# An encoder layer on one core: squares and the rotary sine product moved from GpSimd to VectorE, softmax rows handled in pairs

## The chip, the cores and the metric

The kernel runs on one core of a Trainium2 chip. The metric is the device time of one execution in microseconds, the median of the runs shown. One further execution was taken by the hardware profiler; its own time stands beside them.

## What is computed

One layer of a bidirectional encoder over 1024 tokens of width 1024, in float32. Cut to what matters:

```python
hn = rmsnorm(x, norm_mix)
qa, ka, va, qb, kb, vb = split(hn @ w_in)         # 8+2+2 heads for group A, 8+8+8 for group B, 64 wide
qa, ka = partial_rope(qa), partial_rope(ka)       # the first 16 of 64 dims are rotated
# group A: sliding window |i-j| <= 128, 4 query heads share a key head, one learned sink logit per head
m = max(max(s), sink); p = exp(s - m); denom = sum(p) + exp(sink - m); o_a = p @ va / denom
# group B: neighbourhood attention on a 16 x 64 token grid, window 8 x 16, learned bias by offset
p = softmax(s + bias); o_b = p @ vb
h = x + concat(rmsnorm(o_a, norm_a), rmsnorm(o_b, norm_b)) @ w_out
hn = rmsnorm(h, norm_ffn)
h = h + (silu(conv3(hn @ w_gate)) * (hn @ w_up)) @ w_down      # conv3: centred, depthwise, width 3; 2816 wide
out = rmsnorm(h, norm_final)
```

## The kernel before

Activations lie transposed in SBUF: features on the 128 partitions, the 1024 tokens along the free axis, eight tiles of 128x1024 for a width of 1024. Every matmul operand is split into a high and a low part (ScalarE rounds the high part, VectorE subtracts it), and each product is three matmuls: high by high, low by high, high by low (`block`, lines 113 to 115). Half a tile of 512 tokens is one bank of PSUM.

**Start (0 to 45 us).** The tiles of x arrive one by one. `split_scaled` makes `xgh` (line 125, ScalarE) and `xgl` (line 126, VectorE). Two projections run over all eight tiles as they come; their four accumulators fill four banks. `load_w` loads weights and splits them (lines 108 and 109). The sum of the squares of x, for the first RMS norm, comes from `squares(xts, nc.gpsimd)`: ScalarE squares a tile (line 139) and the engine that is named adds it to the sum (line 141), seven adds of 128x1024. A third projection starts before the norm is known. Then the partition sums (line 150), the inverse root and its spreading over all partitions (`widen`, line 161) give `rstd1`, by which every projection is multiplied when it leaves its bank (`evacuate`, line 170).

**Projections and attention (45 to 400 us).** Each projected tile goes through `post`. The tiles of group A's queries and keys (six of them) are rotated by `rotate`: two DMAs issued from ScalarE's queue copy the partner rows into a tile `u` (line 182; two such tiles take turns), VectorE multiplies the tile by the cosines (line 183), GpSimd multiplies `u` by the sines (line 184), and VectorE adds the two (line 185). `split_pair` (lines 190 to 195) then makes the two query operands, with three DMAs on SyncE's queue, and `split_k` the keys.

Attention goes by rows: one row is one head's 128 queries against 256 or 384 keys. `scores` makes two matmuls (line 266) into one of two banks named `s`. `softmax` follows: GpSimd copies the negated sink logit into a spare column (line 283, group A alone), VectorE subtracts the scores from the mask or bias, writes them into `p` and finds the row's extremum (line 284), ScalarE takes the exponential and its sum (line 288), VectorE inverts the sum (line 289), GpSimd scales the row (line 290). Two rows share one tile `p`. Then TensorE transposes `p` (line 322 in group A, 395 in group B), ScalarE and VectorE split the transposed tile into `ph` and `pl` (lines 295, 296), and TensorE multiplies them with the values (lines 327 and 328, or 406 and 407). In group A a unit has the four heads of one key head at one block, 16 units in all; in group B a unit has two rows, 32 units.

**The order.** TensorE's order is written out by hand. The score rows run up to two units ahead of the transposes, and between these steps `fill` puts in blocks of the projections that later units need, at rates that a table `RATES` sets. The order on the other engines is made by a scheduler at build time from dependencies and priorities; `softmax` runs at raised priority. Each engine then executes its list in that order.

**Output projection and MLP (400 to 1135 us).** These use TensorE, VectorE and ScalarE, and GpSimd four times at the very end.

Of the kernel before, what the change touches and what calls it, by code (L numbers as in the profile page):

```python
# [13 lines left out]
F32 = mybir.dt.float32  # L14
F32R = mybir.dt.float32r
AF = mybir.ActivationFunctionType
ALU = mybir.AluOpType
# [34 lines left out]
def hybrid_layer(tc, xT, w_in, w_out, w_gate, w_up, w_down, small, sink, rpb, consts, rope, out):  # L52
    nc = tc.nc
    with ExitStack() as ctx:
# [9 lines left out]
        spool = inner("stats", 6)  # L64
# [6 lines left out]
        def tmp(name, dt=F32, n=S):  # L71
            return tpool.tile([128, n], dt, name=name, tag="t", padded_shape=[128, S + 2])
# [62 lines left out]
        def squares(tiles, engine):  # L135
            acc = None
            for t in tiles:
                s2 = tmp("sq")
                nc.scalar.activation(s2, t, AF.Square)
                if acc is not None:  # L140
                    engine.tensor_tensor(s2, s2, acc, op=ALU.add)
                acc = s2
            return acc
# [34 lines left out]
        def rotate(t, n):  # L178
            u = turned[0]
            turned.append(turned.pop(0))  # L180
            for i in (0, 4):
                nc.scalar.dma_start(u[i:n:8], t[4 - i:n:8])
            nc.vector.tensor_tensor(t[0:n], t[0:n], rc[0:n], op=ALU.mult)
            nc.gpsimd.tensor_tensor(u[0:n], u[0:n], rs[0:n], op=ALU.mult)
            nc.vector.tensor_tensor(t[0:n], t[0:n], u[0:n], op=ALU.add)

        def split_pair(t):
# [86 lines left out]
                return lpool.tile([128, 2, 386], F32, name="p", tag="mix", bufs=slots["mix"], padded_shape=[128, 2, 512])  # L274
            return apool.tile([128, 2, 386], F32, name="p", tag="p", bufs=5)

        def softmax(p, j, ps, n, bias, nsink=None):

            w = lambda ap: ap.rearrange("p (c w) -> p c w", w=128)
            with tc.high_priority(offset=50):  # L280
                nm, sm = spool.tile([128, 1], F32, name="nm"), spool.tile([128, 1], F32, name="sm")
                if nsink is not None:
                    nc.gpsimd.tensor_copy(p[:, j, n:n + 1], nsink)
                nc.vector.tensor_tensor_reduce(  # L284
                    out=w(p[:, j, 0:n]), in0=w(ps[:, 0:n]), in1=bias, scale=1.0, scalar=3e38 if nsink is None else nsink,
                    op0=ALU.add, op1=ALU.min, accum_out=nm)
                e = n if nsink is None else n + 1
                nc.scalar.activation(p[:, j, 0:e], p[:, j, 0:e], AF.Exp, bias=nm, scale=-1.0, accum_out=sm)  # L288
                nc.vector.reciprocal(sm, sm)  # L289
                nc.gpsimd.tensor_scalar(p[:, j, 0:n], p[:, j, 0:n], sm, 1.0, op0=ALU.mult, op1=ALU.mult)  # L290

        def split_pt(ps, n):
            ph = apool.tile([128, HALF], F32R, name="ph", tag="ph")
# [5 lines left out]
        def unit_window(g, b):  # L299

            cs, n = near(b), 128 * len(near(b))
            ps4 = [None] * 4
            mask = cst[:, K_MA:K_MA + 384].rearrange("p (c w) -> p c w", w=128)
            mask = mask[:, cs[0] - b + 1:cs[-1] - b + 2]
            st = {}

            def q_step(j):
                def go():
                    if j % 2 == 0:
                        st["p"] = pair_tile(True)  # L310
                    ps, _ = scores(qa[g, j // 2][j % 2], ka[g], b)
                    softmax(st["p"], j % 2, ps, n, mask, nsink[:, 4 * g + j:4 * g + j + 1])
                    ps4[j] = st["p"][:, j % 2, :]
                return go

            def t_step(i):
                def go():
                    if i == 0:
                        st["o"] = bank("o", "o")
                    pt = bank("pt", "pt")  # L320
                    for j in range(4):
                        nc.tensor.transpose(pt[:, j * 128:(j + 1) * 128], ps4[j][:, i * 128:(i + 1) * 128], ident)
                    ph, pl = split_pt(pt, HALF)

                    def v_step():
                        o, v = st["o"], va[g]
                        nc.tensor.matmul(o, v[:, cs[i], :], ph, start=i == 0, stop=False)
                        nc.tensor.matmul(o, v[:, cs[i], :], pl, start=False, stop=i == len(cs) - 1)
                        if i == len(cs) - 1:
                            leave()  # L330
                    return v_step
                return go

            def leave():
                ot = apool.tile([128, 2, 128], F32, name="ot", tag="ot", bufs=1, padded_shape=[128, 4, 128])
                o4 = st["o"][:, :].rearrange("p (j w) -> p j w", w=128)
                for e in range(2):
                    me, other = slice(64 * e, 64 * e + 64), slice(64 - 64 * e, 128 - 64 * e)
                    nc.scalar.activation(ot[me], o4[other, e::2, :], AF.Copy)
                    for i in range(2):  # L340
                        if mix[2 * g + i] is None:
                            mix[2 * g + i] = big("mixa", "mix")
                        nc.vector.tensor_tensor(mix[2 * g + i][me, b * 128:(b + 1) * 128], o4[me, e + 2 * i, :], ot[me, i, :], op=ALU.add)

            return [q_step(j) for j in range(4)], [t_step(i) for i in range(len(cs))]
# [19 lines left out]
        def units_grid(h):  # L365

            ps4 = [None] * NB
            st = {"begun": [False, False]}
            e = 64 * (h % 2)
            me, other = slice(e, e + 64), slice(64 - e, 128 - e)  # L370

            def q_step(b):
                def go():
                    if b == 0:
                        bias_of[h] = bias_of.pop(h, None) or bias_tiles(h)
                    if b == 4 and h < 7:
                        bias_of[h + 1] = bias_tiles(h + 1)
                    x = bias_of[h]
                    if b % 2 == 0:
                        st["p"] = pair_tile()  # L380
                    sel = slice(2, 5, 2) if b == 0 else slice(0, 3, 2) if b == NB - 1 else slice(1, 4)
                    ps, n = scores(qb[h], kb[h], b)
                    softmax(st["p"], b % 2, ps, n, x[:, sel, :])
                    ps4[b] = st["p"][:, b % 2, :]
                return go

# [111 lines left out]
        xts, sqs = [], []  # L498
# [42 lines left out]
        nsink = cpool.tile([128, 8], F32, name="nsink")  # L541
        nc.vector.tensor_scalar(nsink, par[:, C_SINK:C_END], -1.0, None, op0=ALU.mult)
        rc, rs = big("rc", "mix"), big("rs", "mix")
# [3 lines left out]
        for _ in range(2):  # L547
            u = big("u", "mix")
# [4 lines left out]
        acc = None  # L553
        for k in range(KT):
            if k:
                xg[k] = split_scaled(xts[k], col(C_NMIX + k), "xg", "xg")
            for h in range(2):
                for p, ps in zip(first, banks):
                    block(ps[h], p.w[k], xg[k], h, k == 0, k == KT - 1)
        acc = squares(xts, nc.gpsimd)  # L560
        jobs = [Project(m) for m in range(2, 18)] + [OutA(d) for d in range(KT)]
        third = jobs[0]
        raw, hi, lo = big("raw3", "mix"), big("whi3", "mix", F32R), big("wlo3", "mix", F32R)
# [184 lines left out]
        for h in range(2):  # L748
            wide = widen(vb2[h], "pt")
            for i in range(4):  # L750
                x = mix[4 + i][:, tsl(h)]
# [93 lines left out]
        for h in range(2):  # L845
            for d in range(KT):
                if h == 0 and d + 2 < KT:
                    wo.append(load_wo(d + 2, fpool))
                ps = bank("pj", ("pj", "o", "s")[(h * KT + d) % 3])
# [264 lines left out]
        for i, f in enumerate(FO[HEAD:]):  # L1114
            u = Gated(f)
# [99 lines left out]
        for i, (p, j, c) in enumerate(order):  # L1215
            prepare(i + 6, i + 4)
            f, n = PARTS[c]
# [4 lines left out]
            ps = banks[p, j]  # L1222
# [120 lines left out]
```

## Time and profile before

| | |
|---|---|
| timed runs | 1141.33 us median of 3 (1141.04 to 1143.16) |
| the profiled execution | 1136.96 us, its span 1135.0 us |
| mean granted TensorE clock | 0.986 of full speed |
| GpSimd: squares, line 141 | 7 adds, 19.6 us |
| GpSimd: sine products, line 184 | 6 products, 16.9 us |
| GpSimd: scaling of rows, line 290 | 128 passes, 77.4 us |
| GpSimd: copies of the sink, line 283 | 64 copies, 13.3 us |
| VectorE: reciprocals, line 289 | 128, 20.1 us |

The span runs from the first to the last instruction of the profiled execution; all durations are from that execution. PE is TensorE, PEld its weight loads, DVE is VectorE, ACT ScalarE, POOL GpSimd, SP SyncE. A timeline row gives the start in us, the duration, engine, line, operation, the tile written and the tiles read, the shape, and in brackets how long the engine stood idle before it and what ended that. A row of grouped instructions has the count, then busy time and the mean of one in ns, then the idle time before. Matmuls overlap in the pipe, so their starts are closer together than their durations are long.

### The profile page before, as it was taken

The numbers are of one execution on the slowest core, as the hardware profiler recorded it, in microseconds if no ns is written. First come the engines' busy times: TensorE is split into PE (matmuls) and PEld (weight loads), VectorE is DVE, ScalarE is ACT, GpSimd is POOL, SyncE is SP. The second block draws the span as 40 slices with busy tenths as digits, with TensorE's granted clock in tenths as the row PEclk, the third lists the DMA queues.
The fourth block names the chain that finished last, engine by engine and source line by source line (L and its number), as shares of the span: only waits on it lengthen the run. The fifth ranks groups of instructions, "written<-read, shape, count | busy, mean of one in ns | idle before, by whom it ended". The sixth has DMA issues, their size and how long they took to land.

```text
span 1135.0 us, 15044 instructions
## 1 busy us (share of the span) xinstructions
PE 1088.1 (96%) x5124; PEld 903.0 (80%) x5124; DVE 874.7 (77%) x1594; ACT 550.2 (48%) x1033; POOL 149.1 (13%) x233
## 2 busy tenths in 40 slices
PE   7989999999999989999899999999999899999995
PEld 5867788888878878888688888888888688888884
DVE  6687888766689667899988778877887778886843
ACT  6235677655767534445443334333433554543531
POOL 4634533233223100000000000000000000000001
PEclk8999999999999999999999999999999999999998
DMA  7242120233305317402542223222322799775723
GB/s 273 72 119 74 48 57 28 73 95 89 78 28 150 101 47 241 146 31 96 192 131 103 107 89 129 94 103 93 123 101 93 232 319 298 260 226 163 261 78 148
DMA packets 65294, 147.17 MB, mean 130 GB/s; under 512 B 7969, under 2 KB 14113, under 8 KB 65217
## 3 DMA queue, kind: packets, MB, share of 16 engines
q1 hardware_dynamic: 56256, 121.17, 34.1%
q10 hardware_dynamic: 8960, 25.04, 5.8%
q8 instruction: 40, 0.66, 0.2%
q14 instruction: 38, 0.30, 0.1%
HBM read 104.37 MB, written 28.57 MB: 117 GB/s over the span
## 4 chain that ended last, share of the span: by engine, by line
PE 82%; DVE 8%; DMA 3%; issue 3%; ACT 2%; POOL 1%; SPq 0%; POOLq 0%; ACTq 0%; DVEq 0%
PE dn L785 6%; PE dn L786 6%; PE dn L787 6%; PE pj L113 6%; PE pj L114 6%; PE pj L115 6%; PE z L785 5%; PE z L787 5%; PE z L786 5%; PE x L785 3%; PE x L786 3%; PE x L787 3%; PE y L787 3%; PE y L785 3%; PE y L786 3%; PE s L266 3%
## 5 line engine op out<-in xcount | busy, mean ns | idle before, releaser
L774 ACT ACTIVATE whi<-ws 128x512 fp32r<-128x512 f32 (+1 forms) x100 | 60.1, 623 | 125.4 <-DVE ws L891 85.5
L785 PE MATMUL dn<-xd,whi 128*128 128x512 f32 x308 | 120.0, 390 | 0.0
L787 PE MATMUL dn<-xd,wlo 128*128 128x512 f32 x308 | 119.8, 389 | 0.0
L786 PE MATMUL dn<-xd,whi 128*128 128x512 f32 x308 | 119.8, 389 | 0.0
L785 PE MATMUL z<-hg,whi 128*128 128x512 f32 x264 | 103.4, 392 | 2.4 <-DVE gs L941 2.4
L787 PE MATMUL z<-hg,wlo 128*128 128x512 f32 x264 | 103.7, 393 | 0.2 <-DVE wlo L775 0.2
L113 PE MATMUL pj<-xgh,whi 128*128 128x512 f32 x248 | 103.8, 418 | 0.0
L786 PE MATMUL z<-hg,whi 128*128 128x512 f32 x264 | 103.3, 391 | 0.0
L290 POOL TENSOR_SCALAR p<-p,sm 128x384 f32<-128x384 f32 (+1 forms) x128 | 77.4, 606 | 192.1 <-DVE sm L289 165.3
L1197 POOL TENSOR_TENSOR y<-y,wide 128x512 f32<-128x512 f32 x4 | 5.1, 1280 | 734.1 <-ACT y L1196 734.1
L288 ACT ACTIVATE p<-p,nm 128x385 f32<-128x385 f32 (+3 forms) x128 | 74.9, 586 | 49.4 <-DVE nm L284 43.9
L114 PE MATMUL pj<-xgl,whi 128*128 128x512 f32 x248 | 97.8, 394 | 0.3 <-DVE xgl L126 0.3
L115 PE MATMUL pj<-xgh,wlo 128*128 128x512 f32 x248 | 98.1, 396 | 0.0
L775 DVE TENSOR_TENSOR wlo<-raw,whi 128x512 fp32r<-128x512 f32 (+1 forms) x102 | 66.5, 671 | 22.1 <-ACT whi L774 21.1
L774 ACT ACTIVATE whi<-raw 128x512 fp32r<-128x512 f32 (+1 forms) x102 | 61.0, 612 | 46.3 <-DMA raw<-in_w_down_dram 11.1
L775 DVE TENSOR_TENSOR wlo<-ws,whi 128x512 fp32r<-128x512 f32 (+1 forms) x100 | 66.9, 681 | 19.8 <-ACT whi L774 19.7
L296 DVE TENSOR_TENSOR pl<-pt,ph 128x384 fp32r<-128x384 f32 (+2 forms) x108 | 63.2, 588 | 21.5 <-ACT ph L295 20.2
L295 ACT ACTIVATE ph<-pt 128x384 fp32r<-128x384 f32 (+2 forms) x108 | 55.3, 514 | 40.6 <-PE pt L395 29.4
L1098 ACT ACTIVATE xd<-xd 128x512 fp32r<-128x512 f32 x77 | 46.9, 626 | 54.1 <-DMA xd<-x 50.7
L787 PE MATMUL y<-hg,wlo 128*128 128x512 f32 x176 | 69.4, 394 | 2.2 <-DVE wlo L775 2.2
L785 PE MATMUL y<-hg,whi 128*128 128x512 f32 x176 | 69.1, 393 | 1.9 <-ACT whi L774 1.9
L785 PE MATMUL x<-hg,whi 128*128 128x512 f32 x176 | 68.8, 391 | 1.4 <-ACT c L925 1.4
(201 smaller groups left out, 2721.9 us busy)
## 6 DMA issues: line engine op xcount, KB each, us to landing
xd<-x SPq DMA_DIRECT2D x77, 256.0 KB, 4.9
raw<-in_w_down_dram SPq DMA_DIRECT2D x72, 256.0 KB, 3.5
raw<-in_w_gate_dram SPq DMA_DIRECT2D x22, 512.0 KB, 3.4
raw<-in_w_up_dram SPq DMA_DIRECT2D x22, 512.0 KB, 5.6
x<-c ACTq DMA_DIRECT2D x22, 512.0 KB, 2.9
raw<-in_w_in_dram SPq DMA_DIRECT2D x32, 256.0 KB, 2.7
raw<-in_w_down_dram SPq DMA_DIRECT2D x36, 192.0 KB, 3.9
x<-t ACTq DMA_DIRECT2D x11, 512.0 KB
```

The source lines that it names most:

```text
L113: nc.tensor.matmul(ps, w[0], x[0][:, tsl(h)], start=first, stop=False)
L114: nc.tensor.matmul(ps, w[0], x[1][:, tsl(h)], start=False, stop=False)
L115: nc.tensor.matmul(ps, w[1], x[0][:, tsl(h)], start=False, stop=last)
L288: nc.scalar.activation(p[:, j, 0:e], p[:, j, 0:e], AF.Exp, bias=nm, scale=-1.0, accum_out=sm)
L290: nc.gpsimd.tensor_scalar(p[:, j, 0:n], p[:, j, 0:n], sm, 1.0, op0=ALU.mult, op1=ALU.mult)
L295: nc.scalar.activation(ph[:, 0:n], ps[:, 0:n], AF.Copy)
L296: nc.vector.tensor_tensor(pl[:, 0:n], ps[:, 0:n], f32(ph[:, 0:n]), op=ALU.subtract)
L774: nc.scalar.activation(hi, src, AF.Copy)
L775: nc.vector.tensor_tensor(lo, src, f32(hi[:, :, :]), op=ALU.subtract)
L785: nc.tensor.matmul(ps, w[0], x[0], start=first and i == 0, stop=False, skip_group_check=True)
L786: nc.tensor.matmul(ps, w[0], x[1], start=False, stop=False, skip_group_check=True)
L787: nc.tensor.matmul(ps, w[1], x[0], start=False, stop=last and i == len(ws) - 1, skip_group_check=True)
```

## The change

The adds of x's squares and the sine product go to VectorE. In `softmax` the two rows that share a tile `p` also share a tile for the sums, 128x2: the sink column of both is copied at once, and when the second row's exponential is done, one reciprocal inverts both sums and GpSimd scales both rows, one after the other.

```diff
@@ -181,7 +181,7 @@
             for i in (0, 4):
                 nc.scalar.dma_start(u[i:n:8], t[4 - i:n:8])
             nc.vector.tensor_tensor(t[0:n], t[0:n], rc[0:n], op=ALU.mult)
-            nc.gpsimd.tensor_tensor(u[0:n], u[0:n], rs[0:n], op=ALU.mult)
+            nc.vector.tensor_tensor(u[0:n], u[0:n], rs[0:n], op=ALU.mult)
             nc.vector.tensor_tensor(t[0:n], t[0:n], u[0:n], op=ALU.add)
 
         def split_pair(t):
@@ -274,20 +274,26 @@
                 return lpool.tile([128, 2, 386], F32, name="p", tag="mix", bufs=slots["mix"], padded_shape=[128, 2, 512])
             return apool.tile([128, 2, 386], F32, name="p", tag="p", bufs=5)
 
-        def softmax(p, j, ps, n, bias, nsink=None):
+        def softmax(st, j, ps, n, bias, nsink=None):
 
             w = lambda ap: ap.rearrange("p (c w) -> p c w", w=128)
+            p = st["p"]
             with tc.high_priority(offset=50):
-                nm, sm = spool.tile([128, 1], F32, name="nm"), spool.tile([128, 1], F32, name="sm")
-                if nsink is not None:
-                    nc.gpsimd.tensor_copy(p[:, j, n:n + 1], nsink)
+                nm = spool.tile([128, 1], F32, name="nm")
+                if j == 0:
+                    st["sm"], st["n"] = spool.tile([128, 2], F32, name="sm"), [n, n]
+                sm, st["n"][j] = st["sm"], n
+                if nsink is not None and j == 0:
+                    nc.gpsimd.tensor_copy(p[:, 0:2, n:n + 1], nsink.rearrange("p (j o) -> p j o", o=1))
                 nc.vector.tensor_tensor_reduce(
-                    out=w(p[:, j, 0:n]), in0=w(ps[:, 0:n]), in1=bias, scale=1.0, scalar=3e38 if nsink is None else nsink,
+                    out=w(p[:, j, 0:n]), in0=w(ps[:, 0:n]), in1=bias, scale=1.0, scalar=3e38 if nsink is None else nsink[:, j:j + 1],
                     op0=ALU.add, op1=ALU.min, accum_out=nm)
                 e = n if nsink is None else n + 1
-                nc.scalar.activation(p[:, j, 0:e], p[:, j, 0:e], AF.Exp, bias=nm, scale=-1.0, accum_out=sm)
-                nc.vector.reciprocal(sm, sm)
-                nc.gpsimd.tensor_scalar(p[:, j, 0:n], p[:, j, 0:n], sm, 1.0, op0=ALU.mult, op1=ALU.mult)
+                nc.scalar.activation(p[:, j, 0:e], p[:, j, 0:e], AF.Exp, bias=nm, scale=-1.0, accum_out=sm[:, j:j + 1])
+                if j == 1:
+                    nc.vector.reciprocal(sm, sm)
+                    for i, m in enumerate(st["n"]):
+                        nc.gpsimd.tensor_scalar(p[:, i, 0:m], p[:, i, 0:m], sm[:, i:i + 1], 1.0, op0=ALU.mult, op1=ALU.mult)
 
         def split_pt(ps, n):
             ph = apool.tile([128, HALF], F32R, name="ph", tag="ph")
@@ -309,7 +315,7 @@
                     if j % 2 == 0:
                         st["p"] = pair_tile(True)
                     ps, _ = scores(qa[g, j // 2][j % 2], ka[g], b)
-                    softmax(st["p"], j % 2, ps, n, mask, nsink[:, 4 * g + j:4 * g + j + 1])
+                    softmax(st, j % 2, ps, n, mask, nsink[:, 4 * g + j - j % 2:4 * g + j - j % 2 + 2])
                     ps4[j] = st["p"][:, j % 2, :]
                 return go
 
@@ -380,7 +386,7 @@
                         st["p"] = pair_tile()
                     sel = slice(2, 5, 2) if b == 0 else slice(0, 3, 2) if b == NB - 1 else slice(1, 4)
                     ps, n = scores(qb[h], kb[h], b)
-                    softmax(st["p"], b % 2, ps, n, x[:, sel, :])
+                    softmax(st, b % 2, ps, n, x[:, sel, :])
                     ps4[b] = st["p"][:, b % 2, :]
                 return go
 
@@ -557,7 +563,7 @@
             for h in range(2):
                 for p, ps in zip(first, banks):
                     block(ps[h], p.w[k], xg[k], h, k == 0, k == KT - 1)
-        acc = squares(xts, nc.gpsimd)
+        acc = squares(xts, nc.vector)
         jobs = [Project(m) for m in range(2, 18)] + [OutA(d) for d in range(KT)]
         third = jobs[0]
         raw, hi, lo = big("raw3", "mix"), big("whi3", "mix", F32R), big("wlo3", "mix", F32R)
```

## The prediction

> **What bounds the kernel now.** I read the busy times and the chain of waits on the page first, then the table of stretches, then the timeline where TensorE idles.
>
> ```profile
> PE 1088.1 (96%) x5124; PEld 903.0 (80%) x5124; DVE 874.7 (77%) x1594; ACT 550.2 (48%) x1033; POOL 149.1 (13%) x233
> PE 82%; DVE 8%; DMA 3%; issue 3%; ACT 2%; POOL 1%; SPq 0%; POOLq 0%; ACTq 0%; DVEq 0%
> 20.00:30.00 10.00, 7.56 (x31) 5.25 (x31) 10.00 (x5) 5.44 (x7) 7.43 (x4) 1.00 0.62 220
> 160.00:180.00 20.00, 20.00 (x107) 17.11 (x106) 17.25 (x52) 13.78 (x34) 7.39 (x22) 1.00 0.32 80
> 480.00:1135.00 655.00, 634.51 (x2803) 523.81 (x2801) 510.99 (x765) 275.38 (x443) 5.12 (x4) 0.99 0.45 151
> ```
>
> A row of stretches has the length, then the busy time of TensorE, its weight loads, VectorE, ScalarE and GpSimd, then the granted clock, the DMA share and GB/s. TensorE sets the end, at 96%. Its order is written out by hand and is the same, instruction for instruction, in the changed kernel as built. So the change can only fill or open holes on TensorE. Nothing that it edits runs behind 480 us: that block shifts as a whole. The holes within its reach are in the first 30 us (VectorE busy 10.00 of 10.00 from 20 to 30), around 77 us, and in the attention; by 160 to 180 there are none.
>
> **The squares.** VectorE gets seven adds of 128x1024. Before, GpSimd made them beside VectorE's splits of x (line 126).
>
> ```profile
> L141 DVE TENSOR_TENSOR sq<-sq x3: 1215/1226/1228, 285.5 to 290.5; 128x1024 f32<-128x1024 f32 x3
> 11.64 1.28 DVE L126 SCALAR_TENSOR_TENSOR xgl<-xt,par,xgh 128x1024 fp32r<-128x1024 f32 x1 [1.84 <-ACT xgh L125]
> 12.63 12.01 POOL L141 TENSOR_TENSOR sq<-sq 128x1024 f32<-128x1024 f32 x4 [11.66 <-ACT sq L139]
> 16.17 2.88 DVE L109 TENSOR_TENSOR wlo<-raw,whi 128x512 fp32r<-128x512 f32 x1
> 18.97 7.94 DVE L126 SCALAR_TENSOR_TENSOR xgl<-xt,par,xgh 128x1024 fp32r<-128x1024 f32 x3
> 26.84 0.68 DVE L109 TENSOR_TENSOR wlo<-raw,whi 128x512 fp32r<-128x512 f32 x1
> ```
>
> And TensorE's idles in the same stretch (start, duration, and in brackets the idle before it and who ended that):
>
> ```profile
> 20.51 0.39 PE L113 MATMUL pj<-xgh,w 128*128 128x512 f32 x1
> 22.44 0.50 PE L114 MATMUL pj<-xgl,w 128*128 128x512 f32 x1 [1.54 <-DVE xgl L126]
> 25.77 0.50 PE L114 MATMUL pj<-xgl,whi 128*128 128x512 f32 x1 [0.32 <-DVE xgl L126]
> 27.57 0.51 PE L115 MATMUL o<-xgh,wlo 128*128 128x512 f32 x1 [0.58 <-DVE wlo L109]
> ```
>
> A split takes 1.28 us when GpSimd is still idle and 7.94 / 3 = 2.65 us beside a GpSimd add; line 109 takes 0.68 alone and 2.88 beside one. Here the two engines slow each other down, GpSimd's adds included: 12.01 / 4 = 3.0 us each. On VectorE an add costs 1.23 us (the row at 285 us). In the order as built, the queue from 11.64 on is split, add, split, line 109, add, split: 1.28 + 1.23 + 1.28 + 0.68 + 1.23 + 1.28 = 7.0 us, so the third split ends near 18.6 to 19. Before, it ended at 18.97 + 2.65 = 21.6, and TensorE wanted it at about 20.7, right behind the row of 20.51. After it come an add and the next two splits, 3.8 us, to about 22.8; TensorE wants the first of them near 23.5. So the three idles go: 1.54 + 0.32 + 0.58 = 2.44 us. Each also made the matmul behind it 0.11 us longer (0.50 against 0.39): 2.44 + 0.33 = **2.8 us**. The last three adds stand behind the last split. Even if that ended no earlier than before (about 32 us), they would be done by 32 + 3.7 = 36 us; the sum of squares is needed only at about 40 (42.9 in the next fence, less 2.8), so these adds are covered.
>
> **The rotation's sine product.** Six products move to VectorE, each right behind the cosine product. The first three are on the way to the first queries:
>
> ```profile
> 42.90 0.95 PE L150 MATMUL ss<-ones,sq 128*128 128x1 f32 x8
> 52.99 5.79 POOL L184 TENSOR_TENSOR u<-u,rs 64x1024 f32<-64x1024 f32 x2 [5.01 <-DMA u<-t]
> 56.47 3.40 DVE L185 TENSOR_TENSOR t<-t,u 64x1024 f32<-64x1024 f32 x1 [1.05 <-POOL u L184]
> 62.13 1.21 DVE L185 TENSOR_TENSOR t<-t,u 128x1024 f32<-128x1024 f32 x1
> 64.47 2.22 DVE L192 SCALAR_TENSOR_TENSOR t<-t,q 128x1024 fp32r<-128x1024 f32 x1 [0.53 <-ACT q L190]
> 72.81 2.37 POOL L184 TENSOR_TENSOR u<-u,rs 64x1024 f32<-64x1024 f32 x1 [7.21 <-DMA u<-t]
> 73.69 2.57 DVE L183 TENSOR_TENSOR t<-t,rc 64x1024 f32<-64x1024 f32 x1
> 77.00 1.21 DVE L185 TENSOR_TENSOR t<-t,u 64x1024 f32<-64x1024 f32 x1
> 78.17 0.48 DVE L284 CUSTOM_DVE_ANT_0 p<-s,cst,nsink 128x256 f32<-128x256 f32 x1
> 77.66 0.36 PE L266 MATMUL s<-ka,q 128*128 128x256 f32 x1 [3.33 <-DMA q<-t]
> 78.72 0.44 PE L266 MATMUL s<-ka,q 128*128 128x384 f32 x1 [0.35 <-DVE nm L284]
> ```
>
> A product costs 1.21 on VectorE (the add at 62.13 has its shape), against 5.79 / 2 = 2.9 on GpSimd, and the add behind it no longer runs beside a product (3.40). The first tile's addition ends at 59.87 now. On VectorE it ends, in the old time scale, at 52.99 + 3 x 1.21 for cosine product, sine product and addition + 0.68 for an eviction of 128x512 between them (the shape of line 109's 0.68) = 57.3: some 2.5 us sooner. A new wait comes with this: the product needs the rows that ScalarE's DMA queue copies into u, and all of VectorE's work stands behind it (evictions, splits, score rows), for which TensorE's banks wait. The rows had landed by 52.99 and VectorE comes to them at about 54.2, behind the cosine product, so it doesn't stop. The rows of the fourth tile land at 72.81, about 70 after the change, and are reached at about 73 (below).
>
> So the DMA of the query tile, which TensorE awaits for 3.33 us at 77.66, lands earlier by 2.8 plus about 2, part of the 2.5 and the 1.0 that line 192 gains (2.22 at 64.47 beside a product), while TensorE arrives 2.8 earlier: this wait shrinks to about 2.3. But it gives nothing, because a new wait stands right behind it. As built, VectorE's queue goes: score rows 0 and 1, cosine product, sine product, addition, row 2; before, the cosine product stood ahead of row 0 and no sine product was there. Rows 0 and 1 cannot start before TensorE's scores at about 73.7 - 2.8 = 70.9 (the 73.69 row began as these ran). Then 2 x 0.41 for the rows, 3 x 1.17 for the three vector passes (77.00 to 78.17, start to start) and 0.41 for row 2: 70.9 + 0.3 + 0.8 + 3.5 + 0.4 = 75.9. TensorE's next scores need the bank that row 2 frees: 78.72 before, 75.9 after, 2.8 us sooner. The whole gain of the squares is kept, and of the faster rotation **0 to 0.5 us**, I take 0.2.
>
> The clock has a part here:
>
> ```profile
> 75.40:78.80 3.40, 0.80 (x5) 0.62 (x5) 3.40 (x10) 1.65 (x5) 0.00 (x0) 1.00 0.36 77
> 78.80:82.20 3.40, 3.40 (x10) 2.77 (x11) 2.98 (x11) 2.09 (x7) 2.11 (x3) 0.56 0.35 77
> ```
>
> Behind 3.40 us in which TensorE was busy for 0.80 the granted clock is 0.56 for 3.4 us, which loses 1.5 us. After the change, two waits of about 2.3 and 2 us stand with 0.5 us of scores between them, as empty as now: I leave this loss in. The Trainium skill, "TensorE: Matmul & The Clock Gate", section "What's actually happening", has the clock fall after at least one idle window of about 3.4 us. By that rule two shorter waits with work between would not trigger it, and the loss would go. The trace does not bear out so strict a reading, since 0.80 us of work did not prevent it.
>
> **The later products.** Two run inside the attention.
>
> ```profile
> 115.58 3.46 POOL L184 TENSOR_TENSOR u<-u,rs 128x1024 f32<-128x1024 f32 x1
> 119.08 1.23 DVE L185 TENSOR_TENSOR t<-t,u 128x1024 f32<-128x1024 f32 x1 [1.17 <-POOL u L184]
> ...
> 100.73 0.41 PE L266 MATMUL s<-ka,q 128*128 128x384 f32 x1 [0.43 <-DVE nm L284]
> 121.47 0.50 PE L328 MATMUL o<-pl,v 128*128 128x512 f32 x1 [1.41 <-DVE pl L296]
> 125.82 0.50 PE L328 MATMUL o<-pl,v 128*128 128x512 f32 x1 [1.03 <-DVE pl L296]
> ```
>
> At 119.08 VectorE waits 1.17 for GpSimd; that wait becomes 1.2 us of work, so the wait at 121.47 stays or grows by about 0.6. Ahead of the one at 125.82 the order as built takes one score row out of the way, and row 10, for which TensorE waits at 100.73, moves ahead of two larger passes. Bounds: all three waits go (2.9 us gained), or the first one doubles (1.4 lost). Nearest are the rows themselves: -0.6 + 1.0 + 0.4 = **0.8 us** gained.
>
> **Rows in pairs.** 64 reciprocals of 128x2 replace 128 of 128x1, and 32 copies of the sink replace 64.
>
> ```profile
> L289 DVE RECIPROCAL sm<-sm 128x1 f32<-128x1 f32 x128 | 20.1, 158 | 16.4 <-ACT p L288 15.0 <-POOL p L283 0.2
> L154 DVE RECIPROCAL v<-v 128x4 f32<-128x4 f32 x2 | 0.3, 173 | 3.6 <-ACT v L153 3.6
> PE pt L322 <- POOL p L290: 0.2, 1, 0.2
> 137.40 0.59 POOL L290 TENSOR_SCALAR p<-p,sm 128x384 f32<-128x384 f32 x1
> 139.13 0.60 PE L322 MATMUL pt<-cst,p 128*128 128x128 f32 x4
> ```
>
> A 128x2 reciprocal is not in the trace; it lies between 158 and 173 ns, so VectorE saves 128 x 0.158 - 64 x 0.17 = 9 us, spread over 300 us in which TensorE waits for VectorE only a few times. Of the nine, 0 to 1.5 us can show; I take 0.5. The price is delay: the pair's first row is scaled only when the second one's exponential is done, so the last row of a unit has another pass of 0.59 us ahead of it on GpSimd. TensorE's transposes have cover for that: at 139.13, among the tightest, they begin 139.13 - 137.99 = 1.14 us after a scaled row that the unit's end needs, and in all the attention TensorE waited for a scale once, for 0.2 us. The delay is hidden there with 0.5 us to spare. The pair's reciprocal also holds VectorE's queue until the second exponential is done. Now that is 15.0 us in all, and with half the reciprocals, as many of them close behind their row, no more than that.
>
> **The sum.** 2.8 + 0.2 + 0.8 + 0.5 = 4.3 us. The profiled execution took 1136.96 (span 1135.0 and 1.96 around it) and should take 1132.7. The median of the timed runs, 1141.33, lies 4.4 above it; the same gain gives **1137.0**. What a measurement of this kernel can tell from no change is about 0.2%, 2.3 us; the three runs shown span 2.1.
>
> **The rivals.**
> *The clock stays full behind the first scores* (0.15). The two new waits have 0.5 us of scores between them, and if that keeps the clock up, or the 3.4 us stretches fall otherwise, 1.5 us more are gained: 1135.5. For it: the wait is cut in two; against: the 0.80 us of work in the row above did not help. By the Trainium skill's page on the clock gate this is the outcome.
> *VectorE takes it back* (0.20). It has 7 x 1.23 + 6 x 1.21 = 15.9 us more to do by 120 us. Against it, the splits alone give back 7 x 1.1. If in the order as built it is late once more, as behind row 1, for the length of two passes (2 x 1.2), and the 0.5 of the pairs does not show: 4.3 - 2.9 = 1.4 gained, 1139.9, no change that can be told.
> *The pairs' delay reaches TensorE* (0.22). GpSimd runs in order; scale passes now come in pairs behind copies that wait for a free tile. Where the cover of a unit's last row is under 0.59 us, TensorE stops for its transposes. It decides if VectorE's pair reciprocals come half a microsecond later than the single ones did, because 1.14 is then eaten. For the 14 window units behind the first two (an estimate), at 0.59 each, that is 8.3 us lost: 1141.33 - 4.3 + 8.3 = 1145.3, slower. For it: VectorE is busy 17.25 of 20 there. Against: the one wait of 0.2.
>
> **How the numbers follow.** The forecast has 0.43; its own range, from the bounds of 0.8 and 0.5 and the 1.5 of the clock, is 1134.5 to 1139.5. Faster by over 0.2% (below 1139.05) are the forecast and the first rival, 0.58; within are the second rival, 0.20; slower is the third, 0.22. The range goes from 1133.5 (first rival with the better bounds) to 1144.5, most of the way into the third rival.
>
> **What would show it.** Right: the splits of x at 1.28 with no idle on TensorE between 20 and 28 us; the first score matmuls near 71; the wait there put down to VectorE's row 2; the products at 1.2 on VectorE; the transposes' waits for line 290's scale still near zero. Wrong: waits of the transposes for GpSimd in most window units, waits of the value matmuls for pl that add up to more than before, or a second stretch at half clock.

## The result, and the profile after

The changed kernel took 1134.65 us (median of six runs, 1133.01 to 1138.03) against 1141.3 for the kernel before (six runs): ratio 0.9947, 95% interval 0.9932 to 0.9963, faster by more than the 0.2%. The forecast was 1137.0. The profiled execution took 1133.92, with a span of 1132.1. In a second series the ratio was 0.9962 (0.9947 to 0.9978). The mean of both, 0.9955, is 5.2 us of 1140, against 4.3 forecast.

The busy times, the chain of waits and the stretches of the changed kernel (columns as in the prediction):

```profile
PE 1088.7 (96%) x5124; PEld 905.5 (80%) x5124; DVE 865.2 (76%) x1543; ACT 550.1 (49%) x1033; POOL 110.6 (10%) x188
PE 87%; DVE 7%; DMA 2%; issue 1%; ACT 1%; SPq 0%; POOL 0%; POOLq 0%; ACTq 0%; DVEq 0%
20.00:30.00 10.00, 10.00 (x46) 8.29 (x45) 7.62 (x9) 5.27 (x7) 2.67 (x4) 1.00 0.66 241
160.00:180.00 20.00, 20.00 (x108) 17.15 (x107) 16.70 (x46) 14.56 (x35) 6.29 (x16) 1.00 0.27 69
480.00:1135.00 655.00, 631.42 (x2787) 520.99 (x2786) 509.71 (x762) 273.56 (x440) 5.11 (x4) 0.98 0.44 150
```

VectorE got thirteen large passes more and is yet busy for 9.5 us less. From 20 to 30 us TensorE is busy for 10.00 where it was 7.56. VectorE's timeline shows why:

```profile
11.72 1.28 DVE L126 SCALAR_TENSOR_TENSOR xgl<-xt,par,xgh 128x1024 fp32r<-128x1024 f32 x1 [1.97 <-ACT xgh L125]
15.25 0.69 DVE L109 TENSOR_TENSOR wlo<-raw,whi 128x512 fp32r<-128x512 f32 x1
18.18 1.22 DVE L141 TENSOR_TENSOR sq<-sq 128x1024 f32<-128x1024 f32 x1
19.32 2.48 DVE L126 SCALAR_TENSOR_TENSOR xgl<-xt,par,xgh 128x1024 fp32r<-128x1024 f32 x2
28.36 3.94 DVE L141 TENSOR_TENSOR sq<-sq 128x1024 f32<-128x1024 f32 x3
```

Every split of x takes 1.28 (2.65 before), line 109 takes 0.69 (2.88), an add of the squares 1.22 (3.0 on GpSimd). The last three adds end at 28.36 + 3.94 = 32.3.

The first scores. TensorE's first partition sum, then VectorE and ScalarE up to row 2 of the scores, and TensorE's two waits:

```profile
40.08 0.95 PE L150 MATMUL ss<-ones,sq 128*128 128x1 f32 x8
51.20 1.21 DVE L184 TENSOR_TENSOR u<-u,rs 64x1024 f32<-64x1024 f32 x1
52.94 1.21 DVE L185 TENSOR_TENSOR t<-t,u 64x1024 f32<-64x1024 f32 x1
57.47 1.21 DVE L185 TENSOR_TENSOR t<-t,u 128x1024 f32<-128x1024 f32 x1
59.85 0.63 ACT L108 ACTIVATE whi<-raw 128x512 fp32r<-128x512 f32 x1 [4.61 <-PE pj L114]
60.39 1.04 ACT L190 ACTIVATE q<-t 128x1024 fp32r<-128x1024 f32 x1
61.47 1.23 DVE L192 SCALAR_TENSOR_TENSOR t<-t,q 128x1024 fp32r<-128x1024 f32 x1 [0.26 <-ACT q L190]
63.74 1.22 DVE L184 TENSOR_TENSOR u<-u,rs 128x1024 f32<-128x1024 f32 x1
65.48 1.22 DVE L185 TENSOR_TENSOR t<-t,u 128x1024 f32<-128x1024 f32 x1
73.87 1.22 DVE L185 TENSOR_TENSOR t<-t,u 64x1024 f32<-64x1024 f32 x1
75.18 0.48 DVE L288 CUSTOM_DVE_ANT_0 p<-s,cst,nsink 128x256 f32<-128x256 f32 x1
74.37 0.55 PE L266 MATMUL s<-ka,q 128*128 128x256 f32 x1 [3.49 <-DMA q<-t]
75.72 0.69 PE L266 MATMUL s<-ka,q 128*128 128x384 f32 x1 [0.16 <-DVE nm L288]
```

The wait for the query tile's DMA did not shrink (3.49, before 3.33). The first partition sum starts at 40.08 instead of 42.90, 2.8 us sooner, and the scores that need row 2's bank at 75.72 instead of 78.72, 3.0 us sooner.

The attention. The value matmuls that wait for VectorE's split pl, the groups of the pairs (busy, mean ns | idle before), and what TensorE waits for in the whole run (total, times, longest):

```profile
95.54 0.50 PE L334 MATMUL o<-pl,v 128*128 128x512 f32 x1 [0.65 <-DVE pl L302]
99.86 0.50 PE L334 MATMUL o<-pl,v 128*128 128x512 f32 x1 [1.05 <-DVE pl L302]
119.00 0.50 PE L334 MATMUL o<-pl,v 128*128 128x512 f32 x1 [1.79 <-DVE pl L302]
L294 DVE RECIPROCAL sm<-sm 128x2 f32<-128x2 f32 x64 | 10.3, 161 | 9.4 <-ACT p L292 8.4 <-POOL p L287 0.3
PE o L334 <- DVE pl L302: 3.5, 3, 1.8
PE s L266 <- DVE nm L288: 0.2, 1, 0.2
```

No transpose waits for a scale. The waits for pl add up to 3.5 us, as before (3.6 in four places).

### The profile page after: what moved, and what is told of

It is laid out like the page before. It is cut to its first block, busy times and chain, and to the rows that moved or that the text cites. A ratio compares the mean times of both kernels' runs of the same rounds, so it can differ in the third digit from the quotient of the medians.

```text
span 1132.1 us, 14903 instructions
## 1 busy us (share of the span) xinstructions
PE 1088.7 (96%) x5124; PEld 905.5 (80%) x5124; DVE 865.2 (76%) x1543; ACT 550.1 (49%) x1033; POOL 110.6 (10%) x188
## 4 chain that ended last, share of the span: by engine, by line
PE 87%; DVE 7%; DMA 2%; issue 1%; ACT 1%; SPq 0%; POOL 0%; POOLq 0%; ACTq 0%; DVEq 0%
PE pj L113 7%; PE pj L114 7%; PE pj L115 7%; PE dn L791 6%; PE dn L792 6%; PE dn L793 6%; PE z L793 5%; PE z L791 5%; PE z L792 5%; PE s L266 3%; PE x L791 3%; PE x L793 3%; PE x L792 3%; PE y L793 3%; PE y L791 3%; PE y L792 3%
```

## The experiments

Each kernel was run in five rounds beside the kernel before. In the table, idle is the time in which no matmul runs on TensorE (dummies count as matmuls), in us, summed from the profiled trace over the stretch named in us of the span (whole: from the first matmul to the last); the clock is the mean granted clock of the timed runs, with its standard error. As 0.001 of it is 0.001 of the span, it stands for at most some 1.1 us. Over the 85 runs of the kernel before in the last three series, a line fitted through time and clock gives less, 0.6 us for each 0.001 (correlation 0.79).

| kernel | median us | ratio (95%) | idle 19-38 | 60-85 | 85-130 | whole | clock |
|---|---|---|---|---|---|---|---|
| before | 1139.6 to 1141.3 | 1 | 2.44 | 4.04 | 4.20 | 35.5 | 0.9827 |
| before, again | 1140.30 | 1.0000 (0.9988-1.0012) | 1.75 | 3.08 | 4.32 | 34.4 | 0.9823 ± 0.0006 |
| the change, first series | 1134.65 | 0.9947 (0.9932-0.9963) | 0 | 3.65 | 3.50 | 31.5 | 0.9830 ± 0.0009 |
| the change, second | 1135.19 | 0.9962 (0.9947-0.9978) | 0 | 3.96 | 3.50 | 32.2 | 0.9825 ± 0.0007 |
| squares alone | 1137.78 | 0.9974 (0.9964-0.9985) | 0 | 3.90 | 4.67 | 33.7 | 0.9829 ± 0.0006 |
| rotation alone | 1142.66 | 1.0021 (1.0007-1.0034) | 2.11 | 3.68 | 3.96 | 34.7 | 0.9786 ± 0.0007 |
| pairs alone | 1141.47 | 1.0018 (1.0004-1.0032) | 2.48 | 4.25 | 3.38 | 35.4 | 0.9815 ± 0.0009 |
| squares and pairs | 1137.58 | 0.9978 (0.9962-0.9994) | 0 | 4.25 | 3.60 | 35.9 | 0.9823 ± 0.0007 |
| squares and rotation | 1137.10 | 0.9975 (0.9961-0.9989) | 0 | 3.97 | 4.16 | 31.9 | 0.9806 ± 0.0006 |
| fill in the first wait | 1131.21 | 0.9928 (0.9905-0.9951) | 0 | 0.64 | 3.50 | 30.1 | 0.9832 ± 0.0008 |
| dummies in it | 1136.64 | 0.9968 (0.9952-0.9985) | 0 | 0.76 | 3.50 | 29.9 | 0.9832 ± 0.0006 |
| dummies, rotation alone | 1141.68 | 1.0013 (0.9998-1.0027) | 2.30 | 3.54 | 1.02 | 32.3 | 0.9803 ± 0.0007 |
| third pass per pair | 1137.53 | 0.9981 (0.9969-0.9993) | 0 | 3.72 | 3.69 | 34.5 | 0.9817 ± 0.0005 |
| fill in later waits too | 1129.41 | 0.9902 (0.9883-0.9920) | 0 | 0.64 | 3.05 | 29.5 | 0.9855 ± 0.0005 |

**The kernel before, again.** No edit. The two first profiles differ by 2.9 us, the medians by 6.6; was the first profile of before a lucky one?

> The kernel before, unchanged, with a second profile. The profiled execution of before took 1136.96 us, 4.3 us less than the median of its timed runs, while the one of the changed kernel took 1133.92, close to its median of 1134.65. Theory A (the profiled execution of before was a lucky one, by the granted clock): this profile takes 1139 to 1143 us, and against the first it has two to four more stretches of 3.4 us at half clock, 1.5 us each, with waits of the same length. Theory B (the timed runs of the changed kernel are the lucky ones, the true gain is the 3 us between the two profiles): this profile is again near 1137. Ratio 1.000 in both.

The ratio was 1.000 (0.9988 to 1.0012), and this profile's span was 1139.7 with a clock of 0.980 and nearly the same idle as the first one of 1135.0 (34.4 against 35.5). The same 5124 matmuls kept TensorE busy for 1093.7 us instead of 1088.1, with ten stretches of 3.4 us at half clock ahead of the last 15 us instead of six. So a single profile carries some 5 us of luck, which here is clock, and the medians are what a gain is read from.

**Squares alone.**

```
-        acc = squares(xts, nc.gpsimd)
+        acc = squares(xts, nc.vector)
```

> Before, with the squares' adds alone on VectorE. By the prediction's first step the three waits between 20 and 28 us go: 2.8 us gained, 1138.5 by the median of before, and the splits of x at 1.28. Rival (VectorE's added work comes out elsewhere, so the parts do not add up): under 1 us gained.

```profile
20.00:30.00 10.00, 10.00 (x46) 8.27 (x45) 7.53 (x9) 5.49 (x6) 3.05 (x5) 1.00 0.57 208
```

1140.0 to 1137.78 is 2.2 us, the ratio gives 3.0 (1.7 to 4.1). TensorE is busy for 10.00 from 20 to 30. The term of 2.8 stands.

**Rotation alone.**

```
-            nc.gpsimd.tensor_tensor(u[0:n], u[0:n], rs[0:n], op=ALU.mult)
+            nc.vector.tensor_tensor(u[0:n], u[0:n], rs[0:n], op=ALU.mult)
```

> Before, with the sine products alone on VectorE. By the prediction 0.2 us at the first scores and 0.8 in the attention, 1 us in all: 1140.3. Rival (the queries come earlier and this counts by itself): 3 us or more gained. Rival (VectorE's queue is the worse place): slower by up to 1.4 us.

It is slower, by 2.4 us, though TensorE idles no more than before. What fell is the clock, 0.9786 against 0.9827. TensorE's timeline has a longer single wait than any of this part before (1.41), and the table of stretches shows what comes behind it:

```profile
99.49 0.40 PE L327 MATMUL o<-ph,v 128*128 128x512 f32 x1
101.80 0.50 PE L328 MATMUL o<-pl,v 128*128 128x512 f32 x1 [1.91 <-DVE pl L296]
98.90:102.30 3.40, 1.49 (x7) 0.92 (x6) 3.22 (x8) 2.62 (x5) 1.15 (x2) 1.00 0.00 1
102.40:105.80 3.40, 3.40 (x13) 2.90 (x12) 1.91 (x6) 1.62 (x4) 0.58 (x1) 0.50 0.79 227
```

There is another such wait of 1.78 at 124 us, again with half the clock behind it.

**Pairs alone.** The softmax of the change, the other two lines as before.

```
+                if j == 1:
+                    nc.vector.reciprocal(sm, sm)
+                    for i, m in enumerate(st["n"]):
+                        nc.gpsimd.tensor_scalar(p[:, i, 0:m], ...)
```

> Before, with the paired softmax rows alone. By the prediction 0 to 1.5 us gained, 0.5 taken: 1140.8. Rival (the delay of the pair's first row reaches TensorE): 2 us or more lost, with waits of the transposes for line 296. Rival (the rest of the measured gain, 6.65 less the 4.3 of the sum, is here): 2 us or more gained.

```profile
122.29 0.50 PE L334 MATMUL o<-pl,v 128*128 128x512 f32 x1 [1.83 <-DVE pl L302]
120.30:123.70 3.40, 1.57 (x10) 1.19 (x9) 3.40 (x8) 2.15 (x4) 2.28 (x5) 1.00 0.09 22
123.70:127.10 3.40, 3.36 (x10) 2.36 (x9) 2.96 (x9) 1.31 (x3) 1.15 (x2) 0.50 0.88 190
```

Slower by 2.0 (0.5 to 3.6). No transpose waits for a scale, and the idle sum is that of before. The clock is lower again, 0.9815, with one wait of 1.83 and a half-clock stretch behind it in the profile; but a difference of 0.0012 is near its error of 0.0009 and stands for 0.7 to 1.3 us, so that the rest of the 2.0 is not explained. Alone, the parts give -3.0 + 2.4 + 2.0 = +1.4; together they gave -5.2. They don't add.

**The change, again.** No edit.

> The changed kernel unchanged, beside more runs of the kernel before. If the gain of the first runs (ratio 0.9947, 6.6 us by the medians) is the change's own, the ratio stays at 0.994 to 0.996. If part of it was how the half-clock stretches happened to fall in those six executions, the gain shrinks towards what TensorE's idle times account for: 4.0 us (35.5 idle before, 31.5 after), ratio 0.9965. In the profile the idle sum of TensorE stays 31 to 32.5 us either way; the number of 3.4 us stretches at half clock (8 in the first profile of the changed kernel, against 6, and 9 in another, of the kernel before) may be anything from 6 to 9.

0.9962, 4.4 us by the medians, idle 32.2. Between the two answers expected, and nothing against the forecast of 4.3.

**Squares and pairs.** The change with the sine product back on GpSimd.

> The changed kernel with the rotation's sine product back on GpSimd: squares and pairs alone. Against the kernel before the parts alone gave -3.0 (squares), +2.0 (pairs). Theory 1, parts add up: 1140.0 - 3.0 + 2.0 = 1139.0, ratio 0.999. Theory 2, the pairs cost time only by where their waits fall against the rotation's: with the products on GpSimd the wait of about 1.8 us near 120 us stays and is followed by a stretch at half clock, so the pairs cost here what they cost alone (1139 again), and the gain of the change comes from rotation and pairs together. Theory 3, pairs cost only in the kernel's old phase, and with the squares 2.8 us ahead they don't: 1136 to 1137, ratio 0.997.

1137.58: beside the squares the pairs cost nothing that shows (squares alone 1137.78). That is nearer to theory 3 (1136 to 1137) than to theory 1 (1139), but with an interval of 1.8 us either way it excludes neither, and the wait of 1.8 near 119 us that theory 2 names is there.

**Squares and rotation.** The kernel before with both lines changed, softmax rows one by one.

> The kernel before with squares and sine product on VectorE, softmax rows one by one. Theory 1, parts add up: 1140.0 - 3.0 + 2.4 = 1139.4, ratio 0.9995. Theory 2, rotation and pairs cancel each other: 1139.4 as well, with the two waits of 1.8 to 1.9 us near 98 and 121 us that rotation alone had, each with a stretch at half clock behind it. Theory 3, rotation costs only without the squares, whose 2.8 us let the products end ahead of the first score rows: 1135.5 to 1137, ratio 0.996, and no such wait near 98 us. Where theory 3 holds for both this and the run without the rotation, pairs and rotation are each worth about nothing beside the squares.

```profile
93.17 1.03 DVE L109 TENSOR_TENSOR wlo<-raw,whi 128x512 fp32r<-128x512 f32 x1 [0.16 <-ACT whi L108]
94.12 0.68 DVE L296 TENSOR_TENSOR pl<-pt,ph 128x512 fp32r<-128x512 f32 x1
94.86 0.50 PE L328 MATMUL o<-pl,v 128*128 128x512 f32 x1 [1.93 <-DVE pl L296]
```

The same two instructions in the changed kernel:

```profile
94.80 0.69 DVE L302 TENSOR_TENSOR pl<-pt,ph 128x512 fp32r<-128x512 f32 x1
96.60 0.68 DVE L109 TENSOR_TENSOR wlo<-raw,whi 128x512 fp32r<-128x512 f32 x1
```

1137.10: beside the squares the rotation costs nothing that shows in time, but the two waits are there (1.93 and 1.78), against theory 3, and the clock is low (0.9806). In VectorE's queue a weight split of 1.03 us stands ahead of pl. In the changed kernel, with the pairs, that same split comes behind pl (96.60 against 94.80), and the wait there is the 0.65 of above. So the part that the pairs play with the rotation is one of order: they take the long wait near 94 us apart. That this order is why the parts do not add up in time is not shown.

**Fill in the first wait.** Six of the twelve projection blocks that follow the first six score rows, put between rows 1 and 2.

```
-        run_q(q_until(1, 4 + AHEAD))
-        fill(FILL1)
+        run_q(q_until(1, 2))
+        fill(6)
+        run_q(q_until(1, 2 + AHEAD))
+        fill(FILL1 - 6)
```

> The changed kernel with six of the twelve projection blocks that TensorE takes after the first six score rows put between rows 1 and 2, into the wait of 3.5 us for the query tile's DMA: 18 matmuls of 0.39 us change place, no work is added or left out. If that wait is a real hole, TensorE's idle between 60 and 85 us falls from 3.65 to under 1 us, and the stretch at half clock behind it (1.5 us lost for each 3.4 us) goes: 2.5 + 1.5 = 4 us, and with two such stretches 5.5, so 1129 to 1131. Rival: the blocks are then missing where they hid the waits on VectorE from 85 to 130 us (3.5 us idle now), and those grow by what the hole gave back: 1134 to 1135, no change against the changed kernel.

```profile
73.66 0.39 PE L115 MATMUL pj<-xgh,wlo 128*128 128x512 f32 x1
73.89 0.28 PE L266 MATMUL s<-ka,q 128*128 128x256 f32 x1
75.16 0.44 PE L266 MATMUL s<-ka,q 128*128 128x384 f32 x1 [0.64 <-DVE nm L288]
```

1131.21, 4.0 us under the changed kernel of the same series. The score row follows the blocks without a gap, 0.64 is left of the two waits, and the waits of 85 to 130 us are what they were (3.50). The hole was real.

**Dummies in the same wait.** Fourteen matmuls whose results are thrown away, no work moved: this keeps TensorE busy and gains nothing else.

```
         run_q(q_until(1, 4 + AHEAD))      # now in two parts, 2 and 2 + AHEAD
+        hold = psum.tile([128, HALF], F32, name="hold", tag="pt")
+        for _ in range(14):
+            nc.tensor.matmul(hold, xg[0][0][:, 0:128], xg[0][0][:, 0:HALF], start=True, stop=True)
```

> The changed kernel with 14 matmuls of 128x512 added between score rows 1 and 2, into a PSUM tile that nothing reads (their results are thrown away): 14 x 0.235 us start to start = 3.3 us of work without use in the wait of 3.5 us for the query tile. Nothing else is moved. If the half-clock stretch at 73 to 75 us (one or two of 3.4 us, 1.5 us lost in each) comes from that wait, it goes and the time falls by 1.5 to 3 us against the changed kernel (1135.2), to 1132 to 1133.7, with TensorE's real work no earlier up to that point. If it belongs to no particular wait, the time stays at 1135 or rises by what the dummies overrun (under 0.5 us).

```profile
70.17 3.36 PE L707 MATMUL hold<-xgh 128*128 128x512 f32 x14
73.91 0.36 PE L266 MATMUL s<-ka,q 128*128 128x256 f32 x1 [0.38 <-DMA q<-t]
```

In this profile no half-clock stretch follows at 74 us. The next begins at 116.5, where neither profile of the changed kernel has one. The time is 1136.64, no gain, and the clock 0.9832 is within its error of the changed kernel's. So the gain of the fill was the useful work in the hole, and taking away the half-clock stretch behind this one wait is not worth a measurable time by itself.

**Dummies in the waits of the rotation alone.** Seven matmuls against zeros in the two value steps with the long waits.

```
+                        vcount[0] += 1
+                        if vcount[0] in (2, 10):
+                            for _ in range(7):
+                                nc.tensor.matmul(o, zero, ph, start=False, stop=False)
```

> The rotation alone (1142.66, 2.4 us slower than before at a mean clock of 0.979 against 0.983) with 7 matmuls against a tile of zeros in each of its two waits of 1.91 and 1.78 us (at 99 and 124 us), between the two value matmuls: they add zero to the result and take 7 x 0.235 = 1.6 us each. Theory A, the rotation alone is slow because those two waits call half-clock stretches: mean clock back to 0.981 to 0.983 and 1138 to 1140, level with or a little below the kernel before. Theory B, the rotation itself costs the time (VectorE's queue): 1142 to 1143, and the clock stays at 0.979.

```profile
97.57 1.77 PE L335 MATMUL o<-ph,zero 128*128 128x512 f32 x7
99.67 0.50 PE L336 MATMUL o<-pl,v 128*128 128x512 f32 x1 [0.33 <-DVE pl L296]
```

The waits are filled (idle 1.02 instead of 3.96), the clock comes back from 0.9786 to 0.9803, and the time from 1142.66 to 1141.68. That is under half of the way, the interval (0.9998 to 1.0027) holds both ends, and the 0.0017 of clock has an error of 0.0010. Theory A is not borne out in full, nor is it excluded. In the profile of the rotation alone two of thirteen half-clock stretches stand behind these two waits, and six behind 400 us, where the kernels do not differ; the two profiles of the kernel before have three and five there. What else lowers the clock with the rotation alone stays open.

**A third pass per pair on GpSimd**, which doubles the pairs' delay.

```
+                        if i == 0:
+                            nc.gpsimd.tensor_scalar(p[:, i, 0:m], p[:, i, 0:m], 1.0, 1.0, op0=ALU.mult, op1=ALU.mult)
```

> The changed kernel with a third pass of GpSimd in every pair, between the two scales (the first row multiplied by 1.0): the second row is scaled another 0.59 us later, 64 times. It doubles the delay that the pairs bring. If the delay is hidden (the transposes' cover, start of the transposes less end of the last scale that they need, is 0.01 us in one unit of the changed kernel, 0.53 in another and 1.2 or more in the rest), the time rises by at most 0.58 + 0.06 = 0.6 us and the transposes wait for GpSimd in two places at most: 1135 to 1136. If the third rival of the prediction was nearly there, most units wait: 14 x 0.59 = 8 us more, 1143.

```profile
PE o L336 <- DVE pl L304: 3.5, 3, 1.8
PE pt L330 <- POOL p L298: 0.2, 1, 0.2
```

With the delay doubled the transposes wait for GpSimd once, 0.2 us. The time, 1137.53, is 2.3 above the second series of the change, with intervals that overlap; idle from 85 to 130 us is 0.2 more, and from 130 to 400 us it is 6.9, as in the second profile of the change. The rest of the 2.3 was not traced to the pass.

**Fill in later waits too.** The version with the filled wait, and one, one and two more blocks between the value matmuls of steps 2, 3 and 10, taken from the blocks behind.

```
+                        n = {2: 1, 3: 1, 10: 2}.get(vcount[0], 0)
+                        fill(n)
```

> The version with six projection blocks in the first wait (1131.2), and four more blocks put between the value matmuls that wait for VectorE: one block (0.7 us) each into the waits of 0.65 and 1.05 us at 88 and 92 us, two into that of 1.80 us at 110 us, taken from the blocks that follow. If these waits are real holes, TensorE's idle from 85 to 130 us falls from 3.5 to 1.0 us and the half-clock stretch at 113 goes: 2.5 to 4 us, 1127.5 to 1129. Rival: VectorE is the bound there (its queue is full from 84 to 94 us), later matmuls wait for it instead, and the time stays at 1131.

```profile
93.43 0.50 PE L340 MATMUL o<-pl,v 128*128 128x512 f32 x1 [0.92 <-DVE pl L302]
111.96 0.50 PE L340 MATMUL o<-pl,v 128*128 128x512 f32 x1 [0.42 <-DVE pl L302]
115.19 0.50 PE L340 MATMUL o<-pl,v 128*128 128x512 f32 x1 [1.71 <-DVE pl L302]
```

1129.41, the fastest here: 0.9902 of before. Of the holes between 85 and 130 us only 0.45 us went. The waits of 0.65 and 1.05 became one of 0.92. The wait of 1.80 became 0.42, and the next value matmul, which before followed without a stop, waits 1.71. So the rival is right on the longest wait: VectorE is late there whatever TensorE does meanwhile. The half-clock stretch at 113 us is gone from this profile, as expected. What else it gained on the version with the first wait filled, 1.8 us with overlapping intervals, goes with a clock of 0.9855.

## Why the prediction held, step by step

- **Squares, 2.8.** Right in place, mechanism and size: the three idles are gone, the splits run at 1.28, the covered adds end at 32.3 (bound 36), the partition sums start 2.8 us sooner, and the part alone gave 3.0 (1.7 to 4.1).
- **Rotation at the first scores, 0.2.** The result is right, and so is the bound named for it: row 2's bank came free 3.0 us sooner, which is 2.8 + 0.2. That it agrees to 0.2 us is luck, since in the second profiles of the two kernels the same row starts at 80.52 and 74.58, 5.9 us apart. One step is wrong, the DMA of the query tile that "lands earlier by 2.8 plus about 2". The first tile's addition did end at 52.94 + 1.21 = 54.15 (forecast 57.3 - 2.8 = 54.5), and the next tile's at 57.47 + 1.21 = 58.7, 4.7 sooner than before. There two things took the lead away. ScalarE, whose split of that tile before began as the addition ended, now took a weight split ahead of it (59.85), and the query split began at 60.39, 1.7 late. And in the tile behind it, the one that TensorE awaits, the sine product is itself a pass of VectorE's on the way (63.74), which the forecast counted in the tiles before and left out there. Its addition came 3.5 us sooner (65.48, before 68.95), and TensorE came 3.4 sooner too, so the wait of 3.33 stayed (3.49), where 2.3 and a new one of 2 behind it were forecast. It cost little, because VectorE's row 2 stood 0.8 us behind the DMA anyway (75.18 against 74.37), as the prediction said.
- **Later products, 0.8.** Idle between 85 and 130 us fell by 0.7. The parts: the wait of 1.41 grew to 1.79 (0.6 forecast, 0.38 came), the one of 1.03 and the 0.43 for row 10 went, as forecast. Not forecast: at 99.86 a wait of 1.05 stands where there was 0.45. The runs of the parts share this out otherwise than the prediction. With the rotation alone idle there fell by 0.24 only, because the wait of 0.69 at 98 us became one of 1.91. With the pairs alone, and the products still on GpSimd, it fell by 0.82: there too the wait of 1.03 is gone and the 1.41 has become 1.83. So the size of this term is partly luck. The step for row 10 holds: its wait is gone with the rotation alone and stays with the pairs alone (0.52).
- **Pairs, 0.5.** VectorE saved 20.1 - 10.3 = 9.8 us on reciprocals (9 forecast), and the pair's reciprocal costs 161 ns (158 to 173 forecast). On TensorE nothing of it shows behind 130 us: idle from 130 to 400 us is 6.0 and 6.9 in the two profiles, 6.1 before. Ahead of that it does, by the 0.82 just named. Alone the pairs were 2.0 slower all the same, in part by the clock. The term was a guess about a queue that does not bound TensorE there, and what the pairs did do, move a weight split behind pl, the sum did not have.
- **The clock.** "I leave this loss in": it stayed. These are stretches of the changed kernel behind the first scores:

```profile
69.90:73.30 3.40, 0.98 (x7) 0.69 (x5) 3.16 (x8) 2.04 (x4) 0.00 (x0) 1.00 0.70 155
73.30:76.70 3.40, 2.17 (x7) 1.91 (x8) 3.20 (x8) 1.92 (x6) 1.88 (x2) 0.51 0.11 23
76.70:80.10 3.40, 3.40 (x10) 2.78 (x9) 1.86 (x6) 1.69 (x5) 0.93 (x2) 0.50 0.71 154
```

  Behind 0.98 us of work in 3.40 the clock falls to half, here for two stretches; in the second profile of the change it was one. The rule of the Trainium skill, "TensorE: Matmul & The Clock Gate", section "What's actually happening", read as a whole window without work, would have kept the clock up. The trace speaks against that reading, in the rotation alone even with 1.49 us of work in the 3.40 before. The first rival is thereby refuted for the two profiles of the changed kernel.
- **VectorE takes it back.** Not on the whole, in the changed kernel: its waits toward TensorE, pl and row maxima, went from 3.6 + 0.8 to 3.5 + 0.2. One wait of the kind appeared (1.05) and one went.
- **The pairs' delay reaches TensorE.** Refuted: no transpose waits for a scale in the changed kernel, and one for 0.2 us with the delay doubled. The cover is thin in one unit alone (0.01 us, transposes at 93 us), 0.53 in another and over 1.2 in the rest.

- **The signs.** Of those named for being right, one did not come: the wait at the first scores is put down to the DMA for 3.49 us and to VectorE's row 2 for 0.16. Of those named for being wrong, one came: a second stretch at half clock, in one of the two profiles.

As a sum of idles the forecast is borne out no closer than this: idle is 35.5 and 34.4 us in the two profiles of the kernel before and 31.5 and 32.2 in those of the changed one, 2 to 4 us less, where 4.0 was forecast (4.3 less the 0.33 of longer matmuls). The medians fell by 6.6 and 4.4; what lies between is not settled by runs of one kernel that scatter by 3 to 9 us. That the rotation and the pairs can each lose 2 us alone and not lose it together was in no step of the prediction; it happened to cancel.

## What to carry to other kernels

Two engines that slow each other down when they work side by side, as VectorE and GpSimd do here (a split of 1.28 us took 2.65), are worth parting even if one of them then does all the work: 7 adds moved, and VectorE was done sooner. Before counting on an operand that is ready earlier, look at the order of every engine on its way, since a scheduler may spend the gain elsewhere. A wait that no faster producer shortens can still be filled with work that is due later: six matmul blocks in another place brought 4 us, nearly as much as the whole change.

## What the runs showed of the hardware that was not expected

The granted clock decides among variants whose idle times agree. Rotation alone idled no longer than the kernel before and ran at 0.9786 instead of 0.9827 in the mean of twelve runs; at 0.6 us for each 0.001 that is 2.5 us, about the 2.4 that it lost (at 1.1 us it would be 4.5). Filling its two waits of 1.8 to 1.9 us brought back 0.0017 of the 0.0041. Two profiles of the same kernel can differ by four stretches of 3.4 us at half clock (1135.0 and 1139.7 us, clock 0.980 in the longer one), so that a difference of 3 us between two profiles says nothing until the timed runs say it too.

How empty a stretch must be for that can be read from the 14 profiles of this case. The clock changes only at the ends of stretches of 3.41 us. Up to 1115 us of the span, and leaving the partition sums of line 150 out of TensorE's time, all 68 stretches at full clock with less than 1.5 us of matmuls were followed by half clock, of those with 1.5 to 1.75 us 16 of 32 were, and of 4331 with more none was. The wait near 120 us lies at this edge. At 1.4 us (both profiles of the kernel before, squares alone) it left 1.85 to 2.03 us of work in its stretch and the clock stayed full. Grown to 1.8 it left 1.58 to 1.63 in seven profiles, and half clock followed in each; in both profiles of the changed kernel it fell across two stretches, the emptier one with 2.1 us of work, and the clock stayed full. So a wait that grows by 0.4 us can cost a stretch at half clock on top, or not, by where the stretches happen to lie.

The partition sums are matmuls with a single column, and time in them seems not to count. In the kernel before they fill TensorE from 405.91 to 409.40 us:

```profile
406.90:410.30 3.40, 3.40 (x28) 3.25 (x28) 0.14 (x1) 1.16 (x3) 0.00 (x0) 1.00 0.00 0
410.30:413.70 3.40, 3.40 (x10) 2.63 (x9) 0.84 (x3) 0.00 (x0) 0.00 (x0) 0.50 0.43 154
```

TensorE is busy for all of the first stretch, and still the clock is half in the next. The same is seen in 11 of the 14 profiles.
